# A two-layer hybrid backbone with streamed experts on one core: float32 output projection, logits from un-normalised rows, and other slots for the weight chunks

## Chip, core and metric

One NeuronCore of a Trainium2 chip runs one program. The metric is device microseconds for one execution, lower is better; the time before is the median of three runs.

## What is computed

Two layers act on 256 latent tokens `x` and 256 context tokens `ctx` of width 1024, in float32. A layer is a mixer (attention, convolution, Fourier and recurrent branches, merged by sigmoid gates) and, after a post-norm, a mixture of 16 experts with a second post-norm. All six modulation vectors of a layer come from `c` (or `c_ctx`) by one matrix `ada_w`. The part that matters here:

```
merged = sum over branches of sigmoid(gate) * (branch @ w_branch)
x1  = layer_norm(alpha * x + gate1 * (merged @ w_out)) * ln1_g + ln1_b
h   = layer_norm(x1) * (1 + scale2) + shift2
aff = softmax(h @ w_router)                 # 16 experts
top_w, top_i = top_k(aff.T, 32)             # every expert picks 32 tokens of each stream
xe  = h[top_i]
ye  = (silu(xe @ w_e_gate) * (xe @ w_e_up)) @ w_e_down * top_w     # inner width 1408
out = layer_norm(alpha * x1 + gate2 * scatter_add(ye)) * ln2_g + ln2_b
```

Layer 0 does this for both streams (four tiles of 128 tokens), layer 1 for `x` alone (two tiles).

## The kernel before, in words

A layer is `mixer(l)` and then `finish(l)`. A scheduling framework orders the instructions of each engine; SP issues the weight loads in its own order and stops at the first one whose slot is not free.

`mixer` ends with `merge(b, br)`, which runs over four quarters q of the output columns: it loads `w_in` and `w_branch` of the quarter (L498, L499), splits them into two halves of precision (ACT L351, DVE L147), multiplies, and adds to `merged`, which lies in `big`.

`finish` then does, in this order:

1. Gate rows: the gate vector is spread over 128 partitions by a matmul of ones with a diagonal (`gate_rows`, tile `gps`, L998). Router weights `wr` are multiplied by the modulation (`wrm`, L1067).
2. The projection `w_out(si, q)`: per stream si and quarter q one load of 1 MB into a slot of ring1, ACT and DVE split weights and `merged` into high and low parts (`woh`, `wol`, `mh`, `ml`), and PE does three single-pass matmuls of 256 columns for each product (L1137, L1139, L1140), 384 in layer 0 and 192 in layer 1. DVE multiplies by the gate, adds the residual, and takes the statistics (L1147 to L1155).
3. `norms` (post-norm and inner norm, DVE L1009, L1010, ACT L269), then `logits`: eight transposes on PE (L1170), a copy out (`zt`), eight products with `wrm` (L1177), a bias, a transpose back.
4. `soft` and `topk`, for each stream alone: softmax, two matmuls that put tokens into columns, a copy into `cur` (L1204), four rounds of max, index and replace (L1213 to L1216), a cast (L1217), a masked copy `dm` (L1219).
5. One-hot matrices (L1239) and `gather`, matmuls with them that put the chosen rows into `xe` (tile `xp`, L1248, evicted at L1253 by DVE and at L1256 by ACT).
6. The experts: gate and up products (tile `p`, L1368), DVE and ACT make `he`, down products (tile `py`, L1406), weighting by DVE (`yt`, L1413). Every fourth expert, rows are scattered back by a matmul; behind the last one (tile `fin`, L1434) statistics and norm follow, and in layer 1 the output.

The expert weights of a layer are 192 chunks of 1408 KB (per expert four of gate, four of up, four of down), all issued by SP in `fetch` (L1093). A chunk takes a slot in one of four pools: ring1 (3, shared with all other weight loads), `ringa` (4 in layer 0, 7 in layer 1), `ringb` (3) and `ringc` (2), 12 and 15 in all. In layer 0 `ringa` is filled during the projection, one chunk each before four of its eight loads; in layer 1 before the last one. `ringb` opens when the projection's tiles are free, `ringc` when the norm's are. Then slots are reused in turn, as PE reads them out.

Some chunks of `ada_w` for layer 1 ("held" ones, of 1.5 MB) are loaded in layer 0's finish into ring slots and multiplied in between (tile `ax`, L207; ACT copy L210; transposes L228; DVE reduction L231).

Of the kernel before, what the change touches and what calls it, by code (L numbers as in the profile page):

```python
# [9 lines left out]
F32 = mybir.dt.float32  # L10
# [29 lines left out]
NRA = (4, 7)  # L40
NRB = (3, 3)
# [57 lines left out]
def hybrid_kernel(ctx: ExitStack, tc: tile.TileContext, out: bass.AP, A):  # L99
# [230 lines left out]

    def mixer(l, tail=None):
# [77 lines left out]
        else:  # L409
# [4 lines left out]
            def front(t):  # L414
                s = t // 2
                z = z2[:, 2 + t % 2, :]
                if s == 0:
                    post_ln(big[:, t, :], lng, lnb, big[:, t, :])
                    ln_act(z, big[:, t, :])
# [69 lines left out]
        def merge(b, br):  # L489
# [3 lines left out]
            for q in range(4):  # L493
# [6 lines left out]
                ada_more(AKEEP[l])  # L500
                for i in range(2):
# [479 lines left out]
        fills.append(merge(0, mbr))  # L981
# [10 lines left out]
    def gate_rows(pool, l, v, s):  # L992
        g = pool.tile([128, D], F32, name=f"gate{s}", tag=f"g{s}")
        for half in range(2):
            ps = pmm("gps")
# [3 lines left out]
            S.activation(out=g[:, 512 * half:512 * half + 512], in_=ps, func=AF.Copy)  # L999
        return g  # L1000
# [12 lines left out]
    def finish(l, merged):  # L1013
# [9 lines left out]
        z2 = mp.tile([128, nt, D], F32, name="z2") if both else big[:, 0:2, :]  # L1023
        idxb = mp.tile([128, ns, NE * CAP], F16, name="idxb")
        wix = mp.tile([128, NE + 8], F32, name="wix")
        iota = mp.tile([128, 2 + SEQ], F32, name="iota")
        nc.scalar.dma_start(out=iota, in_=A["k_iota"])
        rst = ExitStack()
        ringa = rst.enter_context(tc.tile_pool(name=f"ringa{l}", bufs=NRA[l], side="right", reuse_waits="tile"))
# [14 lines left out]
        cur = rp.tile([64, 256], F32, name="cur")  # L1044
        lnx = ExitStack()
# [6 lines left out]
        shw = np_.tile([128, ns, NE], F32, name="shw")  # L1052
        shb = np_.tile([16, 2], F32, name="shb")
        wpx = ExitStack()
        wp = wpx.enter_context(tc.tile_pool(name=f"wout{l}", bufs=1, side="left", reuse_waits="tile"))
        wrs = wp.tile([128, KD, NE], F32, name="wrs")
        mp2 = mp.tile([128, 16, 2], F32, name="mp2")
        pq = ptp()
        for h in range(2):
            for kk in range(2):  # L1060
# [4 lines left out]
                      in_=pq[:, 0:32].rearrange("p (k a s) -> p a k s", k=2, s=2))  # L1065
        for si, s in enumerate(streams):
            V.tensor_tensor(out=wrm[:, si], in0=wr, in1=md[:, 32:40, s:s + 1].to_broadcast([128, KD, NE]), op=ALU.mult)  # L1067
            V.tensor_tensor(out=wrs, in0=wr, in1=md[:, 24:32, s:s + 1].to_broadcast([128, KD, NE]), op=ALU.mult)
            V.tensor_reduce(out=shw[:, si, :], in_=wrs.rearrange("p k e -> p e k"), axis=AX.X, op=ALU.add)
            sp = ptp()  # L1070
            T.matmul(sp[0:16, 0:1], lhsT=shw[:, si, :], rhs=ones[:, 0:1], start=True, stop=True)
            V.tensor_copy(out=shb[:, si:si + 1], in_=sp[0:16, 0:1])
        mh = wp.tile([128, KD, N], F32R, name="mh")
        ml = wp.tile([128, KD, N], F32R, name="ml")

        def halves(j):
            S.activation(out=mh[:, j, :], in_=merged[:, j, 0:N], func=AF.Copy, scale=0.5)
            V.scalar_tensor_tensor(out=ml[:, j, :], in0=merged[:, j, 0:N], scalar=0.5, in1=mh[:, j, :].bitcast(F32),
                                   op0=ALU.mult, op1=ALU.subtract)

        chunks = []
        for e in range(NE):
            for name in ("w_e_gate", "w_e_up"):
                for kc in range(4):
                    chunks.append(A[name][l, e, 256 * kc:256 * kc + 256, :].rearrange("(p k) n -> p (k n)", k=2))
            dn = A["w_e_down"][l, e].rearrange("(p k) n -> p (k n)", k=FF // 128)
            for kc in range(4):
                chunks.append(dn[:, MSLOT * kc:MSLOT * kc + MSLOT])
        ready = []

        def fetch():
            v = slot()[:, 0:MSLOT]
            nc.sync.dma_start(out=v, in_=chunks.pop(0))  # L1093
            ready.append(v)

        def chunk():
            if not ready:
                fetch()
            return ready.pop(0)

        if both:
            y = z2
        else:
            y = big[:, 2:4, :]
        stats = {}
        gate1 = {}

        def w_out(si, q):
            s = streams[si]
            v = load(A["w_out"][l], KD, [(256 * q, 256 * q + 256)])  # L1110
            if both and q == 0:
                name = ("ctx", "x")[s]
                nc.sync.dma_start(out=z2[:, 2 * s:2 * s + 2, :], in_=A[name][0].rearrange("(t p) d -> p t d", p=128))
            if both and (si, q) in ((0, 1), (0, 3), (1, 1), (1, 3)):
                prefetch(ringa, 1)
            if not both and q == 3:
                prefetch(ringa, NRA[l])
            c = slice(256 * q, 256 * q + 256)
            ps = pax("wo").rearrange("p (i c) -> p i c", i=2)
            for k0 in (0, 4):  # L1120
                wh = wp.tile([128, 4, 256], F32R, name="woh", bufs=2)
                wl = wp.tile([128, 4, 256], F32R, name="wol", bufs=2)
                for k in (0, 2):
                    if si == 0 and q == 0:
                        halves(k0 + k)
                        halves(k0 + k + 1)
                    src = v[:, k0 + k:k0 + k + 2, :]
                    S.activation(out=wh[:, k:k + 2, :], in_=src, func=AF.Copy)
                    lo_part(V, wl[:, k:k + 2, :], src, wh[:, k:k + 2, :])
                if si == 0 and q == 0 and k0 == 0:  # L1130
                    for g in streams:
                        gate1[g] = gate_rows(wp, l, 2, g)
                for i in range(2):
                    tt = slice(128 * (2 * si + i), 128 * (2 * si + i) + 128)
                    for k in range(4):
                        o = ps[:, i, :]
                        T.matmul(o, lhsT=mh[:, k0 + k, tt], rhs=wh[:, k, :], start=(k0 + k == 0 and i == 0), stop=False,  # L1137
                                 skip_group_check=True)
                        T.matmul(o, lhsT=mh[:, k0 + k, tt], rhs=wl[:, k, :], start=False, stop=False, skip_group_check=True)  # L1139
                        T.matmul(o, lhsT=ml[:, k0 + k, tt], rhs=wh[:, k, :], start=False, stop=(k0 + k == KD - 1),  # L1140
                                 skip_group_check=True)
            if q == 0:
                stats[si] = [small.tile([128, 4, 6], F32, name="st") for _ in range(2)]
            tm = wp.tile([128, 2, 256], F32, name="tm", tag="tm", bufs=2)
            g1 = gate1[s][:, c]
            if q < 3:
# [18 lines left out]
        def logits(si, i):  # L1165
# [14 lines left out]
            if i == 0:  # L1180
                lgt[si] = pmm("lgt")
# [338 lines left out]
```

## Time and profile before

| what | us |
|---|---|
| median of three runs (2405.01 to 2407.66) | 2406.28 |
| the profiled execution | 2407.04 |
| its span, from the first to the last instruction | 2405.3 |
| PE busy | 2039.1 (85%) |
| PE weight loads busy (beside PE) | 1203.1 (50%) |
| DVE busy | 1009.3 (42%) |
| ACT busy | 638.9 (27%) |

The mean granted clock of TensorE is 0.901 of 2.4 GHz. The program moves 713 MB, 296 GB/s over the span. PE, PEld, DVE, ACT, POOL are the engines of the profile; "SPq" rows are DMA issues of SP, whose duration is the time that SP spent on them, with the waits between if a row merges several. A row "x4" merges four instructions. A name in brackets with an arrow is what ended the idle time. A float32 matmul is two instructions in these rows, a single-pass one is one.

### The profile page before, as it was taken

To read this page: it belongs to the slowest core of one execution; us is meant where nothing else is said; L and a number is where in the kernel's file an instruction comes from. 1 tells how busy PE (TensorE), PEld (TensorE's weight loads), DVE (VectorE), ACT (ScalarE), POOL (GpSimd) and SP (SyncE) were. 2 spreads that over 40 slices of the span, in tenths; PEclk is the share of its full clock that TensorE was granted. 3 is DMA by queue.
4 is the path that set the end of the run, shared out by engine and by line. 5 is a ranking of instruction groups with operands and counts; after the bars stand their busy time and mean duration, and the time that the engine had idled before them with its cause. 6 is when DMAs were issued, how large, how long until landed. Compare 5 with 4: busy or idle time off the path is not lost.

```text
span 2405.3 us, 35167 instructions
## 1 busy us (share of the span) xinstructions
PE 2039.1 (85%) x14813; PEld 1203.1 (50%) x14813; DVE 1009.3 (42%) x2063; ACT 638.9 (27%) x1165; POOL 42.5 (2%) x112
## 2 busy tenths in 40 slices
PE   7999999999989897897988798899976766767665
PEld 4877777767844332332432487788942211312111
DVE  5878855563851131311211777897641110101102
ACT  4355555453420000000000447766410000000000
POOL 1010000000000000000000000000000000000000
PEclk9999999999999999999999999999986665766668
DMA  9564533314589999999999584343799999999997
GB/s 282 162 188 149 177 102 114 90 62 172 167 314 423 419 423 423 423 422 422 423 423 422 152 257 151 98 126 117 275 369 423 423 423 423 423 423 423 424 422 302
DMA packets 226781, 713.07 MB, mean 296 GB/s; under 512 B 34428, under 2 KB 174188, under 8 KB 177472
## 3 DMA queue, kind: packets, MB, share of 16 engines
q1 hardware_dynamic: 219696, 703.37, 75.6%
q0 software_dynamic: 2528, 3.99, 0.5%
q10 hardware_dynamic: 4400, 3.47, 0.5%
q8 instruction: 116, 1.90, 0.3%
q14 instruction: 41, 0.34, 0.0%
HBM read 709.74 MB, written 1.05 MB: 296 GB/s over the span
## 4 chain that ended last, share of the span: by engine, by line
DMA 46%; PE 41%; DVE 6%; ACT 5%; issue 1%; ACTq 0%; DVEq 0%; SPq 0%
DMA wslot<-in_w_e_down_dram 16%; DMA wslot<-in_w_e_up_dram 15%; DMA wslot<-in_w_e_gate_dram 14%; PE mm L150 6%; PE mm L152 6%; PE mm L151 6%; PE p L1368 4%; PE py L1406 2%; PE pp L152 2%; PE pp L150 2%; PE pp L151 2%; PE ax L207 1%; PE sc L928 1%; PE po L953 1%; PE wo L1139 1%
## 5 line engine op out<-in xcount | busy, mean ns | idle before, releaser
L1368 PE MATMUL p<-wslot,xe 128*32 128x352 f32 x6144 | 609.4, 541 | 163.1 <-DMA wslot<-in_w_e_gate_dram 86.4
L1368 PEld LDWEIGHTS p<-wslot,xe 128*32 128x32 f32 x6144 | 201.9, 121 | 558.3 <-issue 256.4
L1406 PE MATMUL py<-wslot,ht 128*32 128x256 f32 (+2 forms) x2176 | 283.9, 492 | 87.1 <-DMA wslot<-in_w_e_down_dram 45.8
L1381 DVE TENSOR_TENSOR he<-he,p 128x352 f32<-128x352 f32 x48 | 24.3, 507 | 677.6 <-PE p L1368 677.6
L150 PE MATMUL mm<-hh,wh 128*128 128x512 f32 (+2 forms) x832 | 296.8, 358 | 6.4 <-ACT wh L351 4.6
L152 PE MATMUL mm<-hh,wl 128*128 128x512 f32 (+2 forms) x832 | 291.7, 351 | 8.8 <-DVE wl L147 8.8
L151 PE MATMUL mm<-hl,wh 128*128 128x512 f32 (+2 forms) x832 | 291.6, 351 | 0.0
L1380 ACT ACTIVATE he<-p 128x352 f32<-128x352 f32 x48 | 22.2, 463 | 964.7 <-PE p L1368 962.6
L351 ACT ACTIVATE wh<-wslot 128x512 fp32r<-128x512 f32 (+1 forms) x288 | 175.5, 624 | 251.3 <-PE mm L151 168.1
L147 DVE TENSOR_TENSOR wl<-wslot,wh 128x512 fp32r<-128x512 f32 (+1 forms) x288 | 193.9, 681 | 110.8 <-ACT wh L351 106.8
L1406 PEld LDWEIGHTS py<-wslot,ht 128*32 128x32 f32 (+1 forms) x2176 | 111.0, 130 | 253.3 <-issue 94.3
L1413 DVE SCALAR_TENSOR_TENSOR yt<-py,wix,gate 32x512 f32<-32x512 f32 (+1 forms) x128 | 78.6, 614 | 304.9 <-PE py L1406 303.4
L150 PEld LDWEIGHTS mm<-hh,wh 128*128 128x128 f32 (+1 forms) x832 | 157.2, 189 | 42.4 <-issue 9.3
L152 PEld LDWEIGHTS mm<-hh,wl 128*128 128x128 f32 (+1 forms) x832 | 157.5, 189 | 33.1 <-DVE wl L147 11.0
L151 PEld LDWEIGHTS mm<-hl,wh 128*128 128x128 f32 (+1 forms) x832 | 157.6, 189 | 24.2 <-issue 3.2
L542 DVE SCALAR_TENSOR_TENSOR conv<-up,prm,conv 128x512 f32<-128x512 f32 (+1 forms) x240 | 146.3, 612 | 2.2
L150 PE MATMUL pp<-bh,wh 128*128 128x512 f32 (+1 forms) x256 | 87.1, 342 | 2.6 <-ACT bh L528 1.4
L152 PE MATMUL pp<-bh,wl 128*128 128x512 f32 (+1 forms) x256 | 86.5, 339 | 1.9 <-DVE wl L147 1.9
L151 PE MATMUL pp<-bl,wh 128*128 128x512 f32 (+1 forms) x256 | 86.2, 337 | 0.0
L1256 ACT ACTIVATE xe<-xp,mp 128x128 f32<-128x128 f32 x48 | 21.9, 457 | 175.2 <-PE xp L1248 96.0
L1139 PE MATMUL wo<-wol,mh 128*128 128x256 f32 x192 | 55.5, 290 | 3.2 <-DVE wol L147 2.8
L1137 PE MATMUL wo<-woh,mh 128*128 128x256 f32 x192 | 55.8, 292 | 0.0
(385 smaller groups left out, 2413.3 us busy)
## 6 DMA issues: line engine op xcount, KB each, us to landing
wslot<-in_w_e_gate_dram SPq DMA_DIRECT2D x128, 1408.0 KB, 27.1
wslot<-in_w_e_up_dram SPq DMA_DIRECT2D x128, 1408.0 KB, 27.1
wslot<-in_w_e_down_dram SPq DMA_DIRECT2D x128, 1408.0 KB, 27.1
wslot<-in_ada_w_dram SPq DMA_DIRECT2D x26, 1536.0 KB, 7.9
wslot<-in_w_in_dram SPq DMA_DIRECT2D x36, 1024.0 KB, 5.4
wslot<-in_w_branch_dram SPq DMA_DIRECT2D x32, 512.0 KB, 6.5
wslot<-in_w_in_dram SPq DMA_DIRECT2D x30, 512.0 KB, 5.8
wslot<-in_w_out_dram SPq DMA_DIRECT2D x12, 1024.0 KB, 5.2
```

The lines of the kernel that those rows point to most:

```text
L147: eng.tensor_tensor(out=lo, in0=src, in1=hi.bitcast(F32), op=ALU.subtract)
L150: T.matmul(o, lhsT=ah, rhs=bh, start=start, stop=False)
L151: T.matmul(o, lhsT=ah, rhs=bl, start=False, stop=False)
L152: T.matmul(o, lhsT=al, rhs=bh, start=False, stop=stop)
L351: S.activation(out=a, in_=v, func=AF.Copy)
L542: V.scalar_tensor_tensor(out=cv, in0=up[:, :, k:k + 256], scalar=pm[:, ct, R_CVW + k:R_CVW + k + 1], in1=cv, op0=ALU.mult, op1=ALU.add)
L1137: T.matmul(o, lhsT=mh[:, k0 + k, tt], rhs=wh[:, k, :], start=(k0 + k == 0 and i == 0), stop=False, skip_group_check=True)
L1139: T.matmul(o, lhsT=mh[:, k0 + k, tt], rhs=wl[:, k, :], start=False, stop=False, skip_group_check=True)
L1368: T.matmul(ts[si][32 * q:32 * q + 32, 0:FB], lhsT=xe[:, k, el, 32 * si:32 * si + 32], rhs=v[:, kk, FB * q:FB * q + FB], start=(k == 0), st ...
L1381: V.tensor_tensor(out=hs, in0=hs, in1=pss[1][si][:, 0:FB], op=ALU.mult)
L1406: T.matmul(py[M * u:M * u + M, c:c + 256 * n], lhsT=ht[:, k], rhs=v[:, 256 * (i - 11 * kc):256 * (i - 11 * kc + n)], start=(k == 0), stop= ...
L1413: V.scalar_tensor_tensor(out=yt[s][32 * el:32 * el + 32, c], in0=py[ps_, 0:dw], scalar=wix[ps_, e:e + 1], in1=gate2[ps_, :], op0=ALU.mult, ...
```

## The change

- **Projection.** `w_out` is loaded once per layer, in four chunks of 512 columns (three in ring1, the fourth, `wo3`, in a tile of its own), and multiplied plainly: float32 matmuls of 512 columns, 64 in layer 0 and 32 in layer 1. Splits, `mh`, `ml` and the stream-wise reloads are gone. The factor 0.5 goes into the gate row. The sum is kept in `y`, in layer 0 a tile of its own.
- **Logits.** Transposes (`turn`) take `y` before the norm. The norm's scale and bias are folded into `wrm` and four constants per expert (`cst`, made by a few DVE operations and one matmul per stream), and four small DVE steps per tile apply mean and reciprocal. `normed`, on ACT, writes the normalised rows for the gather.
- **Softmax and top-k** run once for both streams, on 48 partitions; both gathers follow it.
- **Slots.** `ringa` 5 and 9, `ringb` 2 and 1. In layer 0 `ringa` opens before the last branch is merged, and `merge` asks for two chunks per quarter (five in all); in layer 1 all nine are asked for behind `w_out`'s loads.
- **Held chunks.** Two in tiles of their own, loaded at the start of the finish, two in ring1 behind the projection.
- **Last chunk** of each layer's stream: three loads (1024, 1024, 768 columns).
- **Last expert of layer 1**: the residual and experts 12 to 14 are added to the result early; the last one's weighting is one step of 128 partitions on DVE (before four of 32), followed by eight matmuls of 256 columns (before four of 512). Its scatter matrix `cml` is made in a spare slot.

```diff
-NRA = (4, 7)
-NRB = (3, 3)
+NRA = (5, 9)
+NRB = (2, 1)
...
+    def fetch():
+        v = slot()[:, 0:MSLOT]
+        src = moe["chunks"].pop(0)
+        for c0, c1 in ([(0, 1024), (1024, 2048), (2048, MSLOT)] if not moe["chunks"] else [(0, MSLOT)]):
+            nc.sync.dma_start(out=v[:, c0:c1], in_=src[:, c0:c1])
+        moe["ready"].append(v)
...
-        def merge(b, br):
+        def merge(b, br, ahead=0):
...
                 ada_more(AKEEP[l])
+                if ahead:
+                    prefetch_a(l, ahead)
...
+        y = mp.tile([128, nt, D], F32, name="y") if both else big[:, 2:4, :]
+        z2 = big if both else big[:, 0:2, :]
+        res = y if both else big
...
+        for half in range(2):
+            for kh in range(2):
+                src = A["w_out"][l, 512 * kh:512 * kh + 512, :]
+                if half and kh:
+                    wpc[kh, half] = wp.tile([128, 4, 512], F32, name="wo3")
+                    nc.sync.dma_start(out=wpc[kh, half], in_=src[:, 512:1024].rearrange("(k p) n -> p k n", p=128))
+                else:
+                    wpc[kh, half] = load(src, 4, [(512 * half, 512 * half + 512)])
...
+        prefetch_a(l, NRA[l])
...
+        for _ in range(2 if both else 0):
+            hl_, hp_ = ada_q.pop(0)
+            hn = sum(c1 - c0 for c0, c1 in hp_)
+            hv = wp.tile([128, KD, 384], F32, name="held", bufs=2)[:, :, 0:hn]
...
+        def w_out(t, half):
+            acc[t, half] = pmm("wo")
+            tt = slice(128 * t, 128 * t + 128)
+            for k in range(KD):
+                T.matmul(acc[t, half], lhsT=merged[:, k, tt], rhs=wpc[k // 4, half][:, k % 4, :], start=(k == 0),
+                         stop=(k == KD - 1))
...
+        def turn(t, j0):
+            tp = ptp()
+            for j in range(j0, j0 + 4):
+                T.transpose(tp[:, 128 * (j - j0):128 * (j - j0) + 128], y[:, t, 128 * j:128 * j + 128], ident)
+            zt = zts[t, j0] = np_.tile([128, 4, 128], F32, name="zt", bufs=4)
+            S.activation(out=zt, in_=tp.rearrange("p (a b) -> p a b", a=4), func=AF.Copy)
...
+            u = lv[:, t, :]
+            V.scalar_tensor_tensor(out=u, in0=cst[:, si, 0, :], scalar=ln1[t][0], in1=lg, op0=ALU.mult, op1=ALU.add)
+            V.scalar_tensor_tensor(out=u, in0=u, scalar=ln1[t][1], in1=cst[:, si, 2, :], op0=ALU.mult, op1=ALU.add)
+            V.scalar_tensor_tensor(out=u, in0=cst[:, si, 1, :], scalar=ln2[t][0], in1=u, op0=ALU.mult, op1=ALU.add)
+            V.scalar_tensor_tensor(out=u, in0=u, scalar=ln2[t][1], in1=cst[:, si, 3, :], op0=ALU.mult, op1=ALU.add)
...
+        for t in range(nt):
+            w_out(t, 0)
+            if t:
+                turn(t - 1, 4)
+            evict(t, 0)
+            if t:
+                norms(t - 1)
+            w_out(t, 1)
+            if t and t < nt - 1:
+                logits(t - 1)
+            turn(t, 0)
+            evict(t, 1)
+        turn(nt - 1, 4)
+        norms(nt - 1)
+        warm(AF.Exp, ln2[nt - 1][1])
+        logits(nt - 2)
+        logits(nt - 1)
+        for r in held:
+            ada_use(*r)
+        held = [ada_load(*ada_q.pop(0)) for _ in range(min(AHELD - 2, len(ada_q)))]
         wpx.close()
...
+                if e == NE - 1 and not both:
+                    V.scalar_tensor_tensor(out=yl, in0=py[:, 0:dw], scalar=wix[:, e:e + 1], in1=gate2, op0=ALU.mult,
+                                           op1=ALU.mult)
+                    break
```

How the order of the engines moves is shown at three places. First SP around layer 0's finish. `w_in` and `w_branch` are the mixer's weights, `w_e_gate`, `w_e_up` and `w_e_down` the expert chunks in the order of the stream. Before:

```order
L498 DMA wslot<-in_w_in_dram 128x8x256
L499 DMA wslot<-in_w_branch_dram 128x4x256
L1093 DMA wslot<-in_w_e_gate_dram 128x2816 x3
L133 DMA wslot<-in_w_out_dram 128x8x256 x3
L1113 DMA z_5051<-in_ctx_dram 128x2x1024
L1113 DMA z_5051<-in_x_dram 128x2x1024
L133 DMA wslot<-in_w_out_dram 128x8x256 x5
L133 DMA wslot<-in_ada_w_dram 128x8x384 x3
L1093 DMA wslot<-in_w_e_up_dram 128x2816
L133 DMA wslot<-in_ada_w_dram 128x8x384
L1093 DMA wslot<-in_w_e_up_dram 128x2816 x3
L1093 DMA wslot<-in_w_e_down_dram 128x2816 x4
```

Now:

```order
L351 DMA wslot<-in_w_e_gate_dram 128x2816 x4
L351 DMA wslot<-in_w_e_up_dram 128x2816
L543 DMA wslot<-in_w_in_dram 128x8x256
L544 DMA wslot<-in_w_branch_dram 128x4x256
L133 DMA wslot<-in_w_out_dram 128x4x512 x3
L1115 DMA wo_5105<-in_w_out_dram 128x4x512
L1120 DMA y<-in_ctx_dram 128x2x1024
L1120 DMA y<-in_x_dram 128x2x1024
L1132 DMA held<-in_ada_w_dram 128x8x384 x2
L133 DMA wslot<-in_ada_w_dram 128x8x384 x2
L351 DMA wslot<-in_w_e_up_dram 128x2816 x3
L351 DMA wslot<-in_w_e_down_dram 128x2816 x4
```

Five chunks instead of one now stand ahead of the last `w_in` and `w_branch`; the eight `w_out` loads are four (the fourth, `wo_5105`, is `wo3`); the residual `y` and the two held chunks follow, and ahead of the other seven of the first twelve chunks (three `up`, four `down`) two `ada_w` loads, where there were four.

Second PE at the start of layer 0's finish, behind the last product of the merge (`pp`). `lnr` holds the norm's scale and bias as rows, `cat` the sums that become the constants. Before:

```order
L152 MATMUL pp<-bh,wl 128x512
L1061 MATMUL tp<-mods_112,c_ident 64x16 x4
L998 MATMUL gps<-dg,ones 128x512 x4
L1137 MATMUL wo<-woh,mh 128x256
L1071 MATMUL tp<-ones,shw 16x1
L1139 MATMUL wo<-wol,mh 128x256
L1140 MATMUL wo<-woh,ml 128x256
L1137 MATMUL wo<-woh,mh 128x256
```

Now:

```order
L152 MATMUL pp<-bh,wl 128x512
L1141 MATMUL tp<-mods_112,c_ident 64x16 x4
L1182 MATMUL wo<-wslot,big 128x512 x2
L1047 MATMUL gps<-dg,ones 128x512 x2
L1182 MATMUL wo<-wslot,big 128x512 x2
L1150 MATMUL tp<-c_ident,lnr 128x16
L1182 MATMUL wo<-wslot,big 128x512 x2
L1047 MATMUL gps<-dg,ones 128x512 x2
L1182 MATMUL wo<-wslot,big 128x512 x2
L1171 MATMUL tp<-cat,ones 128x64
L1182 MATMUL wo<-wslot,big 128x512 x4
```

The projection starts before the gate rows, in products of 512 columns, and the matmuls of the constants (`cat`) stand between them.

Third DVE in layer 0, from the copy of the scores into `cur` on. `tp` in `adared` rows is a held chunk's result, `pb` the spread indices, `xe` a step of the gather. Before, for the second stream:

```order
L1204 COPY cur<-pa 16x256
L1213 MAX wi<-cur 16x8
L231 TENSOR_REDUCE adared<-tp 128x6
L1214 MAX_INDEX ix<-wi,cur 16x8
L237 TENSOR_TENSOR mods_121<-adared,adab_117 128x6
L1239 TENSOR_SCALAR oh<-pb,iota 128x128
L1216 MATCH_REPLACE cur<-wi,cur 16x256
L1239 TENSOR_SCALAR oh<-pb,iota 128x128
L1213 MAX wi<-cur 16x8
L1253 TENSOR_SCALAR xe<-xp,mp_5091 128x4x32
L1214 MAX_INDEX ix<-wi,cur 16x8
L1216 MATCH_REPLACE cur<-wi,cur 16x256
```

Now, for both streams:

```order
L1267 COPY cur<-pa 16x256 x2
L1274 MAX wi<-cur 48x8
L1275 MAX_INDEX ix<-wi,cur 48x8
L1277 MATCH_REPLACE cur<-wi,cur 48x256
L1274 MAX wi<-cur 48x8
L231 TENSOR_REDUCE adared<-tp 128x6
L1275 MAX_INDEX ix<-wi,cur 48x8
L237 TENSOR_TENSOR mods_121<-adared,adab_117 128x6
L1277 MATCH_REPLACE cur<-wi,cur 48x256
L1274 MAX wi<-cur 48x8
L1275 MAX_INDEX ix<-wi,cur 48x8
L231 TENSOR_REDUCE adared<-tp 128x6
```

The steps of the gather (`oh`, `xe`) stood between those of the top-k; now all of them stand behind it.

## Rows read from the trace of the kernel before

**Rows 1.** The page, part 4: the chain that ended last, shares by engine and line.

```profile
DMA 46%; PE 41%; DVE 6%; ACT 5%; issue 1%; ACTq 0%; DVEq 0%; SPq 0%
```

**Rows 2.** Windows: busy us of PE, PEld, DVE, ACT, POOL, then PEclk, DMA share, GB/s.

```profile
705.00:1330.00 625.00, 548.47 (x5092) 225.48 (x5092) 119.66 (x224) 33.11 (x65) 6.55 (x13) 0.99 1.01 419
1336.00:1340.00 4.00, 3.31 (x8) 1.12 (x6) 3.92 (x7) 0.00 (x0) 0.00 (x0) 1.00 1.04 328
1743.00:1753.00 10.00, 0.39 (x3) 0.26 (x2) 9.62 (x20) 2.02 (x4) 0.00 (x0) 0.61 0.89 356
```

**Rows 3.** Timeline of SP, layer 0: start, us, engine, line, operation, tiles, count.

```profile
704.13 11.23 SPq L1093 DMA_DIRECT2D wslot<-in_w_e_gate_dram  x4
717.40 2.69 SPq L1093 DMA_DIRECT2D wslot<-in_w_e_up_dram  x2
```

**Rows 4.** Chain of waits, layer 0's finish: start, us, what.

```profile
662.72 0.76 DVE tm L1153 x2
...
674.14 1.97 PE tp L1170 x8
...
682.17 1.92 PE lg L1177 x16
...
689.35 0.43 DVE cur L1204
...
698.57 0.17 DVE wi L1217
...
704.05 1.14 PE xp L1248 x8
...
705.19 2.50 PE p L1368 x30
```

**Rows 5.** Timeline of PE's weight loads after layer 0's last chunk.

```profile
1337.44 0.19 PEld L1434 LDWEIGHTS fin<-yt,cm 128*128 128x128 f32 x1 [0.24 <-issue]
1337.87 0.19 PEld L1434 LDWEIGHTS fin<-yt,cm 128*128 128x128 f32 x1 [0.24 <-issue]
```

**Rows 6.** Timeline of PE: first instruction of layer 0's finish.

```profile
592.07 0.43 PE L1061 MATMUL tp<-mods,c_ident 128*64 128x16 f32 x8
```

**Rows 7.** Timeline of DVE: router weights of layer 0, idle before and releaser in brackets.

```profile
601.48 0.29 DVE L1067 TENSOR_TENSOR wrm<-wr,mods 128x128 f32<-128x128 f32 x1 [1.88 <-DMA wr<-in_w_router_dram]
```

**Rows 8.** Chain of waits, layer 1's finish: start, us, what.

```profile
1718.20 1.91 PE gps L998 x4
...
1743.17 0.76 DVE tm L1153 x2
...
1746.85 1.30 DVE big L1010
...
1748.17 1.30 DVE st L253 x2
...
1762.50 0.20 DVE rmx L1193
...
1764.52 0.43 DVE cur L1204
...
1770.46 0.18 DVE wi L1217
```

**Rows 9.** Timeline of SP, layer 1: the last two free slots and first reuses.

```profile
1746.46 30.84 SPq L1093 DMA_DIRECT2D wslot<-in_w_e_gate_dram  x4
```

**Rows 10.** Timeline of ACT: last quarter of layer 0's merge, first split.

```profile
567.47 0.63 ACT L351 ACTIVATE wh<-wslot 128x512 fp32r<-128x512 f32 x1 [1.60 <-PE pp L151]
```

**Rows 11.** Timelines: PE and DVE behind the last chunk of layers 0 and 1.

```profile
1331.98 2.79 PE L1406 MATMUL py<-wslot,ht 128*64 128x256 f32 x12 [0.65 <-DMA wslot<-in_w_e_down_dram]
...
2389.72 1.50 PE L1406 MATMUL py<-wslot,ht 128*32 128x256 f32 x22 [1.90 <-DMA wslot<-in_w_e_down_dram]
...
2391.28 2.00 DVE L1413 SCALAR_TENSOR_TENSOR yt<-py,wix,gate 32x256 f32<-32x256 f32 x4 [12.25 <-PE py L1406]
```

**Rows 12.** The page, part 6: DMA issues, KB each, us to landing.

```profile
wslot<-in_w_branch_dram SPq DMA_DIRECT2D x32, 512.0 KB, 6.5
```

More of the change, by code (lines that the diff above doesn't have):

```diff
@@ L980, in mixer @@
             ic.__exit__(None, None, None)
-        fills.append(merge(0, mbr))
+        if both:
+            moe_stream(l)
+        fills.append(merge(0, mbr, 2 if both else 0))
         fill(100)
@@ L1089, in finish @@
[L1089 to L1146, printed above, removed]
-                V.tensor_tensor(out=tm, in0=ps, in1=g1.unsqueeze(1).to_broadcast([128, 2, 256]), op=ALU.mult)
-                yq = y[:, 2 * si:2 * si + 2, c]
-                V.scalar_tensor_tensor(out=yq, in0=yq, scalar=ALPHA, in1=tm, op0=ALU.mult, op1=ALU.add)
-            for i in range(2):
-                yq = y[:, 2 * si + i, c]
-                if q == 3:
-                    V.tensor_tensor(out=tm[:, i, :], in0=ps[:, i, :], in1=g1, op=ALU.mult)
-                    V.scalar_tensor_tensor(out=yq, in0=yq, scalar=ALPHA, in1=tm[:, i, :], op0=ALU.mult, op1=ALU.add)
-                V.bn_stats(out=stats[si][i][:, q, :], in_=yq)
@@ new lines, in norms @@
+        def norms(t):
+            mean, r = ln1[t]
+            x1 = y[:, t, :]
+            V.scalar_tensor_tensor(out=x1, in0=x1, scalar=mean, in1=lng, op0=ALU.subtract, op1=ALU.mult)
+            st = np_.tile([128, 2, 6], F32, name="stx", bufs=2)
+            for a in range(2):
+                xa = x1[:, 512 * a:512 * a + 512]
+                V.scalar_tensor_tensor(out=xa, in0=xa, scalar=r, in1=lnb[:, 512 * a:512 * a + 512], op0=ALU.mult, op1=ALU.add)
+                V.bn_stats(out=st[:, a, :], in_=xa)
+            ln2[t] = moments(st, "x")
@@ new lines, in finish, with logits @@
+        lv = rp.tile([128, nt, NE], F32, name="lv")
+        def logits(t):
+            si = t // 2
+            lg = pax("lg")[:, 0:NE]
+            for j in range(KD):
+                T.matmul(lg, lhsT=zts[t, j // 4 * 4][:, j % 4, :], rhs=wrm[:, si, j, :], start=(j == 0), stop=(j == KD - 1))
+            u = lv[:, t, :]
[3 more added lines that the diff above has]
+            V.scalar_tensor_tensor(out=u, in0=u, scalar=ln2[t][1], in1=cst[:, si, 3, :], op0=ALU.mult, op1=ALU.add)
@@ L1204, in soft @@
-            V.tensor_copy(out=cur[r0:r0 + 16, :], in_=pa[r0:r0 + 16, 0:256])
-            return af[:, 1, 0:1]
-        def topk(si):
-            s = streams[si]
-            r0 = 32 * s
-            ix = rp.tile([64, CAP], U32, name="ix", bufs=2)
+            for t in range(nt):
+                r0 = 32 * streams[t // 2]
+                T.matmul(pa[r0:r0 + 16, 128 * (t % 2):128 * (t % 2) + 128], lhsT=af[:, t, :], rhs=ident, start=True,
+                         stop=True, skip_group_check=True)
@@ L1386, in finish @@
                             total[t, c.start] = pmm("fin")
-                            T.matmul(total[t, c.start], lhsT=ident, rhs=big[:, t, c], start=True, stop=False)
+                            for h in range(1 if both else 2):
+                                d = c if both else slice(c.start + 256 * h, c.start + 256 * h + 256)
+                                o = total[t, c.start][:, d.start - c.start:d.stop - c.start]
+                                T.matmul(o, lhsT=ident, rhs=res[:, t, d], start=(h == 0), stop=False, skip_group_check=not both)
                 if e == 0:
```

273 lines of the change are left out of this document (164 added, 109 removed).

## Prediction

> **What bounds the kernel now.** The chain that ended last, summed by engine, comes first: it is almost half DMA, by far the most of it expert weights, and 41% PE [rows 1]. So two kinds of time count: the weight streams, and what runs on PE, DVE and ACT before a stream is at full speed or after it has ended. Second, the windows: in layer 0's stream, 705 to 1330, the 16 DMA engines are never free and move 419 GB/s, while PE at a granted clock of 0.99 is busy 548 of 625 us [rows 2]. A chunk of 1408 KB at that rate is 3.44 us. There, nothing but an earlier start or a shorter end helps.
>
> When does the stream start? Twelve chunks fit into the slots of layer 0 (fifteen in layer 1); SP issues the next one when PE has read the first out of its slot. The SP rows give these releases: the first four chunks from 704.13, the next at 717.40 [rows 3]. The four cover 13.27 us, about their 13.8 us of DMA, and from there PE frees a slot faster than DMA fills one (the four's rows of PE are 2.50 us of expert matmuls and 1.14 us of gather each [rows 4]). **So the issue at 717.40 is the mark: as much earlier as it comes, so much earlier layer 0 ends.** What leads up to it are the projection (last column out at W = 662.72), the router chain (scores in `cur` at 689.35), the top-k (through at 698.57), and gather and first chunks [rows 4].
>
> **The projection.** Before: three single-pass matmuls per product, with the splitting on ACT and DVE. After: plain float32 matmuls of 512 columns, 64 in layer 0 and 32 in layer 1. The trace has that shape at layer 0's end: one float32 matmul is two instructions, and their weight loads start 0.43 us apart [rows 5], in a window whose granted clock is 1.00, the 2.4 GHz level [rows 2]. So one costs 0.86 us. The Trainium skill (TensorE: Matmul & The Clock Gate, Back-to-back issue gap) counts N/2.4 + 2.5 ns for N columns at the full clock, 216 ns here, and no more for float32; by it the projection would be half as long. The row says double that; I go by the row, and the page's figure is the last rival.
>
> Layer 0 from 592.07, where PE begins the finish [rows 6]: 64 x 0.86 = 55.0; four gate matmuls 3.4; six groups of four transposes at 1.0 (eight instructions took 1.97 at one place [rows 4], where PE had just been idle; that is the other end) 6.0; logits of two tiles at 1.92 [rows 4] 3.8; constants 0.7. One new wait: PE stands in order behind the matmul of the folded constants, which needs `wr` (DVE got it at 601.48, after 1.88 us of waiting for it) and some ten small DVE operations at 0.29 [rows 7], so 604.4. PE, with eight projection and four gate matmuls in front, is there by 603. I take 2.5 us for it and other small waits; ends 0 and 6, the latter if the loads of `y` and of the held chunks, new on SP's queue at that time, push `wr` back. Sum 592.1 + 55.0 + 3.4 + 6.0 + 3.8 + 0.7 + 2.5 = **663.5, 0.8 later** than before. The splits that vanish from ACT and DVE are worth nothing in themselves: PE sets the pace.
>
> Layer 1 from 1718.2 [rows 8]: gate rows 1.9, 32 x 0.86 = 27.5, two groups of transposes 2.0, constants 0.7: 1750.3 where it was 1743.17, **7.1 later**.
>
> **The router chain.** Before, norm, transposes and logits of the last tiles follow one another behind W: 689.35 - 662.72 = 26.6 us in layer 0, 1764.52 - 1743.17 = 21.4 in layer 1 [rows 4, 8]. After, the transposes take the un-normalised rows and the norm enters the logits as four small DVE steps, so transposes and logits lie beside the norm. What remains behind W on DVE, by layer 1's rows: eviction, three steps like its first of 0.76, 2.1; moments with ACT's root 0.8, two scalings at 1.30, statistics 1.30 [rows 8], moments again 0.8; up to eight logit steps at about 0.2 between them, 1.6; softmax to the copy 1764.52 - 1762.50 = 2.0 [rows 8] and the copy 0.43. That is 11.6. In layer 0 a second copy, reductions of the two held chunks that stand ahead of the last reciprocal in DVE's order, and their waits for PE bring it to 15.5 (ends 13 and 21: the reductions free, or PE's held matmuls at half clock); in layer 1 I take 12.8. So the chain is **11.1 shorter in layer 0, 8.6 in layer 1**.
>
> **Top-k, gather, first chunks.** Layer 0 did top-k for each stream, the first stream's gather interleaved with the second's top-k: 9.2 us from the copy to its end [rows 4]. Now one top-k holds both streams, 5.9 us as in layer 1 (1764.52 to 1770.46 [rows 8]) and 0.3 for two adaLN reductions: 3.0 saved. But the first stream's gather loses its cover: one-hots and masks of two streams behind it, 1.2; the first eviction, 0.9; and PE must do 16 instead of 8 gather instructions ahead of each of the first four chunks, 4 x 1.14 = 4.6 [rows 4]. Net 3.7 lost. Layer 1 has one stream and does what it did.
>
> So the mark of layer 0 moves by 11.1 - 0.8 - 3.7 = **6.6 earlier**, that of layer 1 by 8.6 - 7.1 = **1.5 earlier** (1777, the end of the fourth issue there [rows 9]).
>
> **Moves on the queues.** Five chunks instead of one go ahead of the last `w_in` and `w_branch` of the mixer: 5 x 3.44 = 17 us of DMA from about 530. I put 0 on it: ACT splits the first of these weights at 567.47 [rows 10], some 15 us after that; if they were late, up to 5 us. The two held chunks in own tiles load at the start of the finish instead of behind it; two more in ring1, then ringb: SP waits there in order, for PE to have used the held chunks. All this ends before the mark, so 0, with the 21 above as the price where not.
>
> **The ends of the streams.** Layer 0's last chunk used to be consumed in one go after landing, 2.79 us [rows 11]; now the last of three pieces holds 3 of 11 blocks: 1.8 saved. Layer 1: 1.50 us likewise [rows 11], 1.1 saved, and four steps of 2.00 us in all, of which the first matmul waited for two, become one of 0.4 to 0.5: 0.5 saved. The eight extra matmuls ahead of it lie in the waits for DMA. Together **3.4** (ends 0 and 4.5). The Trainium skill (DMA: Bandwidth & Descriptors, Bandwidth) wants at least 1 MiB per transfer and gives 78% of the peak at 1 MB, 32% at 64 KB; pieces of 384 to 512 KB would lie between, and by that most of the 3.4 would go. The trace's 512 KB loads take 6.5 us to landing beside other traffic [rows 12]; the pieces are queued right behind full transfers, and I take no loss.
>
> **The sum.** 6.6 + 1.5 + 3.4 = 11.5 us. Profiled execution 2407.04, which is 0.76 above the median of the three runs: 2407.04 - 11.5 - 0.76 = **2394.8**, 0.5% below 2406.28.
>
> **Rivals.** All hang on one thing: which share f of the chain's shortening is real. Total gain = (11.1 + 8.6)f - 0.8 - 3.7 - 7.1 + 3.4 = 19.7f - 8.2. About 0.2%, 4.8 us, is what can be told from no change.
> - *Forecast*, f above 0.66: gain over 4.8. For it: transposes and logits stood on the chain one after the other, at a lowered clock. With the ends of the other terms (wait 0, gathers hidden, chain 13): 2386.
> - *Given back*, f from 0.17 to 0.66: about 2406. PE would be nearly empty behind W, as in 1743 to 1753, where it was busy 0.39 of 10 us and the granted clock 0.61, a mix of the two levels [rows 2]; logits, held matmuls and gather would then take up to twice their time.
> - *Slower*, f under 0.17: 2409 to 2414.5, at f = 0. One mechanism: the chain behind the projection is set by DVE's steps and hand-overs between engines, which remain, the transposes were beside it anyhow; then layer 1 pays its 7.1 us in full and layer 0 its lost cover. It decides where less than 3.4 of 19.7 us is saved. Against it: in layer 1 the DVE finishes its norms and then PE's transposes and logits follow, up to the softmax at 1762.50.
> - *Page's rate*: matmuls at 0.216 us would end the projection 27 and 14 us earlier; the gain would be some 50, about 2354. The weight loads speak against it.
> - *Not as it says*: the pieces of the last chunk land together; 2398, inside the forecast.
>
> **Chances.** Forecast 0.67, given back 0.19, slower 0.12, page's rate 0.02. So faster 0.69, same 0.19, slower 0.12. The range leaves out the page's rate, the lowest tenth and the worst of the slower case: 2385 to 2409.
>
> **What would show it.** Right: weight loads of `wo` 0.43 us apart; projection ends near 663.5 and 1750; `cur` copied near 679 and 1763; top-k of 6 us; fifth issue past the slots near 711, in layer 1 the first at 1775; after the last landing 1.8 and 1.6 us less. Wrong: projection instructions near 0.2 us; a DVE wait for PE of many us in front of the softmax; SP late with chunks in front of the first releases; `merge` waiting for `w_in`.

## The result, and the profile after

The changed kernel takes 2393.33 us (median of five runs, 2391.43 to 2394.99) against 2406.28: the ratio is 0.9946 with a 95% interval of 0.9935 to 0.9957. The forecast was 2394.8, with a range of 2385 to 2409. The profiled execution is one of 2391.89 us, with a span of 2390.1. Two later executions, one of `oldlast` (2484.54 us) and one of the kernel before (2680.80 us), showed a lower mean granted clock (0.789 and 0.722) than all others (0.895 to 0.907) and are left out of every median below.

The chain that ended last, on the page, now has more PE than DMA [rows 1]:

```profile
PE 44%; DMA 43%; DVE 6%; ACT 5%; issue 1%; ACTq 0%; DVEq 0%; SPq 0%
```

The windows (columns as in [rows 2]) are layer 0's stream, in a window set 6 us to the left of that in [rows 2], and the ten microseconds behind layer 1's projection.

```profile
699.00:1324.00 625.00, 546.53 (x5087) 226.19 (x5089) 119.47 (x223) 33.11 (x65) 6.54 (x13) 0.99 1.00 419
1739.00:1749.00 10.00, 5.11 (x38) 4.76 (x36) 8.12 (x25) 4.14 (x9) 0.00 (x0) 0.66 0.79 304
```

The stream itself is what it was: PE 547 of 625 us, 419 GB/s. In the second row PE, which had 0.39 us of work there [rows 2], has 5.11: the logits now lie beside DVE's norm.

Layer 0's projection, in timelines: first PE's weight loads, then PE and DVE at its start.

```profile
616.72 0.19 PEld L1182 LDWEIGHTS wo<-wslot,big 128*128 128x128 f32 x1 [0.24 <-issue]
617.15 0.19 PEld L1182 LDWEIGHTS wo<-wslot,big 128*128 128x128 f32 x1 [0.24 <-issue]
```

```profile
590.52 0.43 PE L1141 MATMUL tp<-mods,c_ident 128*64 128x16 f32 x8
...
602.26 0.29 DVE L1162 TENSOR_TENSOR wrp<-wr,mods 128x128 f32<-128x128 f32 x1 [5.42 <-DMA wr<-in_w_router_dram]
...
605.05 0.41 PE L1171 MATMUL tp<-cat,ones 128*128 128x64 f32 x2 [3.07 <-DVE cat L1160]
```

The loads are 0.43 us apart, as forecast. PE waits 3.07 us for the constants. From here to the first reuse of a slot, first the chain of waits, then DVE in a timeline, then SP:

```profile
590.72 11.52 DMA wr<-in_w_router_dram
...
605.46 5.18 PE wo L1182 x8
...
610.81 3.49 PE wo L1182 x8
...
654.74 6.87 PE wo L1182 x16
661.61 0.44 PE tp L1230 x4
662.05 2.58 PE lg L1240 x24
...
674.43 0.83 PE pa L1264 x6
...
683.18 0.18 DVE wi L1278
...
685.34 2.07 PE xp L1312 x8
...
688.05 1.71 PE xp L1312 x8
```

```profile
672.08 0.18 DVE L231 TENSOR_REDUCE adared<-tp 128x6 f32<-128x24 f32 x1 [2.19 <-PE tp L228]
672.18 0.15 DVE L1193 RECIPROCAL rsx<-sdx 128x1 f32<-128x1 f32 x1
...
675.58 0.84 DVE L1267 COPY cur<-pa 16x256 f32<-16x256 f32 x2 [1.30 <-PE pa L1264]
...
678.97 0.18 DVE L231 TENSOR_REDUCE adared<-tp 128x6 f32<-128x24 f32 x1 [0.60 <-PE tp L228]
...
681.60 0.18 DVE L231 TENSOR_REDUCE adared<-tp 128x6 f32<-128x24 f32 x1 [0.56 <-PE tp L228]
```

```profile
650.90 3.80 SPq L133 DMA_DIRECT2D wslot<-in_ada_w_dram  x2
658.21 13.69 SPq L351 DMA_DIRECT2D wslot<-in_w_e_up_dram  x3
677.78 4.85 SPq L351 DMA_DIRECT2D wslot<-in_w_e_down_dram  x4
697.93 10.64 SPq L351 DMA_DIRECT2D wslot<-in_w_e_gate_dram  x4
710.60 0.33 SPq L351 DMA_DIRECT2D wslot<-in_w_e_up_dram  x1
```

Sixteen instructions, eight matmuls, take 6.87 us: 0.859 each. W is 661.6. A held chunk's reduction (`adared`) stands ahead of the last reciprocal (`rsx`), and two more stand between steps of the top-k, which runs from the copy into `cur` (675.58) to the cast into `wi` (683.18). The mark, the fifth issue into a reused slot, has moved from 717.40 to 710.60 [rows 3].

Layer 1: the chain of waits, SP, and the end of the program (timeline of PE and DVE).

```profile
1707.72 1.72 PE gps L1047 x4
...
1731.85 6.87 PE wo L1182 x16
...
1739.15 2.59 PE lg L1240 x24
...
1750.42 0.43 DVE cur L1267
...
1756.29 0.18 DVE wi L1278
```

```profile
1702.28 7.27 SPq L351 DMA_DIRECT2D wslot<-in_w_e_gate_dram  x4
...
1711.98 29.56 SPq L351 DMA_DIRECT2D wslot<-in_w_e_down_dram  x4
1741.62 22.04 SPq L351 DMA_DIRECT2D wslot<-in_w_e_gate_dram  x4
```

```profile
2375.86 0.63 PE L1481 MATMUL py<-wslot,ht 128*32 128x256 f32 x6 [0.34 <-DMA wslot<-in_w_e_down_dram]
2376.55 0.48 DVE L1485 SCALAR_TENSOR_TENSOR wslot<-py,wix,gate 128x256 f32<-128x256 f32 x1 [10.03 <-PE py L1481]
2377.19 3.69 PE L1519 MATMUL fin<-wslot 128*128 128x256 f32 x16 [0.69 <-DVE wslot L1485]
```

W, the end of the last projection group, is 1738.7 here. From the gate rows to the first reuse (the fourth issue of the last row) it was 1718.20 to about 1777.0 [rows 8, 9], 58.8 us; now it is 1707.72 to 1763.3, 55.6 us.

### The profile page after: what moved, and what is told of

Its sections match the earlier page's. It is cut to its first block, busy times and chain, and to the rows that moved or that the text cites. A ratio compares the mean times of both kernels' runs of the same rounds, so it can differ in the third digit from the quotient of the medians.

```text
span 2390.1 us, 34384 instructions
## 1 busy us (share of the span) xinstructions
PE 2046.7 (86%) x14473; PEld 1176.3 (49%) x14473; DVE 972.6 (41%) x1996; ACT 604.3 (25%) x1104; POOL 46.0 (2%) x119
## 4 chain that ended last, share of the span: by engine, by line
PE 44%; DMA 43%; DVE 6%; ACT 5%; issue 1%; ACTq 0%; DVEq 0%; SPq 0%
DMA wslot<-in_w_e_up_dram 17%; DMA wslot<-in_w_e_down_dram 14%; DMA wslot<-in_w_e_gate_dram 10%; PE mm L150 6%; PE mm L152 6%; PE mm L151 5%; PE p L1428 4%; PE py L1481 4%; PE wo L1182 3%; PE pp L152 2%; PE pp L150 2%; PE xp L1312 2%; PE pp L151 2%; PE ax L207 1%; PE sc L975 1%
## 5 line engine op out<-in xcount | busy, mean ns | idle before, releaser
L1312 PEld LDWEIGHTS xp<-oh,big 128*128 128x128 f32 x384 | 57.5, 222 | 35.5 <-issue 16.9
L1312 PE MATMUL xp<-oh,big 128*128 128x128 f32 x384 | 67.3, 325 | 6.8 <-ACT xe L1320 3.8
```

Source lines behind the costliest of these rows:

```text
L1312: T.matmul(ps[:, 0:128], lhsT=z2[:, 2 * si + i, 256 * (j // 2) + j % 2:256 * (j // 2) + 256:2], rhs=oh[i], start=(i == 0), stop=(i == 1))
```

## The experiments

All times are medians; the kernel before had 2405.0 to 2406.6 beside them. What a run shows is read against the changed kernel's 2393.33 and, where a microsecond counts, in its trace. A distance inside a trace is counted from the first instruction of that layer's finish, where the executions differ in front of it: from there to layer 0's mark the kernel before took 125.3 us, and the changed kernel takes 120.1.

**Scatter first.** `before2` is the kernel before once more, for a second profile.

> The kernel before, unchanged, for a second profile. The distance of 1.6 us that the two profiles have by 26 us, where nothing differs, and the 2.3 us that they gain in layer 1's mixer, where the order is the same, are then scatter of single executions: the second profile has them shifted by a microsecond or more. If they belong to the change, it repeats the first within 0.3 us at both places.

It took 2402.65 us (one run; span 2400.9). It stands 1.6 us ahead of the first profile by 28 us, and gains 2.2 more in layer 1's mixer, just as the changed kernel does. So differences of this size come with single executions and need not be the change's. Its SP rows:

```profile
703.06 11.23 SPq L1093 DMA_DIRECT2D wslot<-in_w_e_gate_dram  x4
716.33 5.06 SPq L1093 DMA_DIRECT2D wslot<-in_w_e_up_dram  x3
```

Its finish begins at 590.5, like the changed kernel's, so the mark moved by 716.33 - 710.60 = 5.7 us. Laid side by side, the changed kernel is 6.4 us ahead at the end of layer 0, 9.7 in layer 1's stream and 10.8 at the end: **layer 0's finish 6.4, layer 1's 3.3, the tail 1.1.** The first profile gives similar pieces, 5.3 for the mark, 3.2 and 1.5, and some 4 us of scatter on top.

Scatter can lie in the finish as well. Three later runs with the same code there (`slots1`, `onepiece`, `oldlast`) take 119.9 to 120.3 us to the mark, as the changed kernel does, but the profiled execution of `half1`, also with the same code in layer 0, takes 123.4. Its granted clock was 0.50, the 1.2 GHz level, from 667 to 672, though PE had been busy without a gap since 655; at the same place (665 to 670) the changed kernel's was 1.00. Eight logit instructions there took 1.82 us instead of 1.03.

**The order of norm and transposes.** `normfirst` puts that one thing back:

```
-            if t:
-                turn(t - 1, 4)
             evict(t, 0)
             if t:
                 norms(t - 1)
+                place(t - 1)          # ACT writes the normed rows into y
...
             if t and t < nt - 1:
+                turn(t - 1, 0)
+                turn(t - 1, 4)
                 logits(t - 1)
-            turn(t, 0)
             evict(t, 1)
...
```

Behind the loop, the transposes and logits of the last two tiles follow their norms in the same way.

> The changed kernel with the order of the finish put back in one respect: the transposes and logits of a tile wait until its rows are normed (one more ACT pass writes the normed rows in place; the arithmetic of the logits is left as it is, so they no longer stand for the reference's). Theory: taking the un-normed rows is what shortens the router chain; behind W two tiles' transposes and logits come back onto it, some 8 us in layer 0 at full price and about as much in layer 1 at half price: 10 to 14 us slower than the changed kernel, 2403 to 2407. Rival, the chain is set by DVE's steps and hand-overs and the gain came from the joint softmax and the slots: at most 3 us, 2393 to 2396.

2410.0 us (2408.52 to 2413.07), 1.0018 of the kernel before (1.0007 to 1.0028): 16.7 us slower than the changed kernel, more than the whole gain, and beyond the range that the theory gave. In the trace, layer 0's mark comes 7.8 us later behind the start of its finish, and layer 1's first reuse 7.7 us later behind its gate rows. Its chain of waits behind layer 0's W:

```profile
669.48 1.25 ACT y L1331
670.77 1.98 PE tp L1230 x8
672.88 0.58 ACT zt L1232
673.51 1.89 PE lg L1240 x8
...
676.82 1.82 PE lg L1240 x8
678.64 4.13 PE ax L207 x30
```

and its windows there:

```profile
661.00:671.00 10.00, 2.93 (x24) 2.60 (x23) 7.35 (x21) 3.20 (x6) 0.00 (x0) 0.67 0.32 133
671.00:682.00 11.00, 10.22 (x53) 6.28 (x55) 1.38 (x6) 6.14 (x8) 0.00 (x0) 0.53 0.00 0
```

First DVE does most of the work, with PE busy 2.93 of 10 us; then PE does, busy 10.22 of 11 us at a granted clock of 0.53 (nearly all of it at the 1.2 GHz level), with groups of eight logit instructions at 1.8 to 1.9 us, where such a group took 1.03 in the changed kernel. DMA moves nothing from 671 to 682, since ringb waits for the held chunks behind the logits. The extra pass on ACT (1.25 us) has its like in the kernel before. So the order of norm and transposes carries the gain: with it put back, the rest of the change comes out 4.3 us slower than the kernel before (2405.74 beside it). How that loss is shared between the projection and the joint top-k, this run does not show.

**The projection's length.** `half0` and `half1` multiply only every other block of `w_out` in one layer, so half of the products are left out; the edit is that of `half0`, `half1` has `l == 1`:

```
-            for k in range(KD):
+            ks = range(0, KD, 2) if l == 0 else range(KD)
+            for k in ks:
```

> The changed kernel, but in layer 0 the projection multiplies only every other block of rows (32 of 64 matmuls; half of the products are left out). Theory, layer 0 is bound by PE there: DMA was idle for 33 us during the projection because every slot was full or not yet free, and slots come free with the projection, so the full 32 x 0.86 = 27.5 us come off the end: 2365 to 2369. Rival, the DMA wall stands in layer 0 too (twelfth chunk landed 696.7, first reuse 697.9, only 8 us idle between): 2383 to 2387.

> The changed kernel, but in layer 1 the projection multiplies only every other block of 128 rows of w_out (16 of 32 matmuls; half of the products are left out). Theory, two walls in layer 1: the fifteenth chunk lands at 1764.0 when the first slot is reused at 1763.3, and the DMA engines were idle for only 2.6 and 0.7 us from 1703 on, so the end cannot come much more than 3.3 us earlier, though PE is 16 x 0.86 = 13.8 us sooner through: 2388 to 2391 where the changed kernel has 2393.3, with DMA never idle and the first reuse waiting. Rival, the chain through projection and router alone sets the start of the stream: 13.8 us earlier, 2379 to 2381.

`half0`: 2367.83 us, 25.5 less, of 27.5: layer 0's start hangs on PE, as the theory had it. `half1`: 2386.62 us, 6.7 less, of 13.8: neither theory nor rival (its four runs lie between 2383.59 and 2391.92, so the share is rough). Its trace stands 4.9 us behind the changed kernel's at layer 1's gate rows; counted from there, the first reuse comes 12.6 us sooner (after 43.2 us instead of 55.8), but the program ends only 7.8 us sooner. Windows of the changed kernel, ahead of the first reuse and around it, then of `half1`:

```profile
1737.00:1741.00 4.00, 4.00 (x27) 3.00 (x26) 2.20 (x7) 2.02 (x3) 0.00 (x0) 1.00 0.03 11
1762.00:1764.00 2.00, 2.00 (x16) 1.00 (x8) 0.04 (x1) 0.00 (x0) 0.00 (x0) 0.83 0.12 49
```

```profile
1708.00:1760.00 52.00, 39.13 (x232) 24.78 (x234) 32.08 (x88) 12.38 (x24) 0.00 (x0) 0.80 1.00 418
```

In the changed kernel DMA stands still for 3.9 and 1.8 us, more than the 2.6 and 0.7 of the expectation. In `half1` these gaps are gone: from 1708 on DMA is full, and what the chain is shorter beyond them is lost. So in layer 1 two bounds stand close together. A longer chain costs its full price (`normfirst`), a shorter one brings half of what it saves, or a little more.

**Slots and early loads.** `slots1` sets layer 1's slots back to 7 and 3, `noahead` takes the early requests out of layer 0's merge:

```
-NRA = (5, 9)
-NRB = (2, 1)
+NRA = (5, 7)
+NRB = (2, 3)
```
```
-        fills.append(merge(0, mbr, 2 if both else 0))
+        fills.append(merge(0, mbr, 0))
```

> The changed kernel with layer 1's slots as before the change: ringa 7 and ringb 3 instead of 9 and 1, so two chunks more wait for the end of the projection. Theory, two walls in layer 1: DMA loses 2 x 3.4 us beside the projection, and the end comes 5 to 7 us later, 2398 to 2401. Rival, layer 1 is bound by the router chain and the loads are hidden: no change, 2392 to 2395.

> The changed kernel with nothing asked for during layer 0's merge; the five ringa chunks are issued in the finish, behind w_out and the residual. Theory: DMA is idle for 33 us during the projection, so the five chunks, 17 us, load there at no cost: within 1.5 us of 2393.3. Rival, the early request is where layer 0's gain comes from: 2400 or more.

2393.45 and 2392.77 us: neither matters. For `noahead` that was the theory. For `slots1` the theory fell: a slot of ring1 takes the eighth chunk during the projection, so only one chunk is later. DMA then stands still for some 5.7 us in one piece, from 1735.3 to 1741, and not again at the first reuse: about as long as the two gaps of the changed kernel together. About 1 us is lost in its trace.

**Room for held chunks.** `noroom` loads all four into ring1 behind the projection:

```
-        for _ in range(2 if both else 0):
+        for _ in range(0):
...
-range(min(AHELD - 2, len(ada_q)))
+range(min(AHELD, len(ada_q)))
```

> The changed kernel without room of their own for held chunks: all four are loaded into ring1 behind the projection. Theory: 3 MB more to load between the projection and the first reuse, 7.3 us, where DMA had 7.9 us of idle, and the last two are used late, so down chunks wait for them: the mark comes 2 to 6 us later, 2395 to 2399, though the router chain loses its held matmuls and DVE's 2.2 us of waiting. Rival, the chain decides: 1 to 3 us earlier, 2390 to 2392.

2391.97 us (0.9946, 0.9933 to 0.9959), span 2390.2: by the medians as the change. The trace is nearer to the rival: the last of the first twelve chunks is issued some 3 us later, but the router chain, without held matmuls ahead of the softmax, is 2.1 us shorter (11.8 us from W to the first copy into `cur`, 13.9 in the changed kernel), and the mark comes after 117.9 us instead of 120.1. Two microseconds are less than the medians tell.

`heldall` and `heldfirst` go the other way and use the held chunks sooner: in `heldfirst` the two in own tiles (the edit shown), in `heldall` also the two in ring1 (ahead of `soft()`).

```
+        for r in held:
+            ada_use(*r)
         turn(nt - 1, 4)
         norms(nt - 1)
         warm(AF.Exp, ln2[nt - 1][1])
         logits(nt - 2)
         logits(nt - 1)
-        for r in held:
-            ada_use(*r)
```

> The changed kernel with the held chunks of ada_w multiplied sooner in layer 0: the two in own tiles right behind the last projection matmul, the two in ring1 before the softmax. Theory: in the changed kernel DVE waits 2.2 us for a held chunk's reduction ahead of the last reciprocal, and SP waits for the same chunks before it can issue ringb and two down chunks (DMA idle 6.5 us); without both the stream starts 2 to 4 us sooner: 2389 to 2391.5. Rival, first reuse and twelfth landing are set by something else (top-k, gather): 2392 to 2394.5.

> The changed kernel with the two held chunks of the own tiles multiplied right behind the last projection matmul, ahead of the last transposes and logits; the two in ring1 stay where they were. Theory after the two runs before: what made that order slow there was ACT, whose root for the last statistics stood behind the copies of the ring1 chunks; without those, DVE's 2.2 us of waiting goes, ringb is issued 4 us sooner, and the mark of layer 0 comes 1 to 2.5 us earlier: 2390.5 to 2392.5, and in the trace the first copy into cur near 673. Rival, another order on ACT or PE gives it back: 2393 or more.

`heldall`: 2397.97 us, 4.6 slower. The wait did not go, it went to another engine. ACT's root of the last statistics stands in its order behind the copies of the ring1 chunks, and the softmax behind a table load (chain of waits):

```profile
675.75 0.49 ACT adapart L210
676.24 0.18 ACT sdx L1191
...
676.44 1.28 ACT L1249
...
679.08 0.64 PE pa L1264 x8
```

`pa`, the softmax's result, comes 4.3 us later than in the changed kernel, once the 0.3 us between the two executions are taken off, and the mark 2.5 us later (122.6 us). The trace is 5.4 us longer than the changed kernel's; most of the rest lies in layer 1's mixer, where both do the same. `heldfirst`, without the wait on ACT, took 2392.77 us (0.9950, 0.9937 to 0.9963): no change that can be told. SP issued ringb at 664 instead of 671 as expected, but `pa` is where it was: PE's logits now come last. The mark comes after 118.0 us, 2.0 sooner, which again is less than the medians tell.

**The gather's cover.** `ctxtopk2` is `heldall` with softmax and top-k of the context stream during the projection of `x`:

```
             evict(t, 1)
+            if both and t == 2:
+                warm(AF.Sqrt, soft(0))
+                topk(0)
+                spread(0)
```

> As heldall, and softmax and top-k of the context stream run during the projection of x, so that the gather of the context stream lies beside the top-k of x again, as before the change. Theory: the prediction's term for the lost cover (3.7 us, of it 4.6 for 16 instead of 8 gather instructions per chunk) is real, and comes back on top of heldall: 2384 to 2388. Rival, DMA is then the bound of the start, or DVE is full during the projection and delays W: no better than heldall.

2394.11 us: as the changed kernel, 3.9 less than `heldall`. `pa` is 4.6 us late here too, yet the mark (710.34) is where the changed kernel has it, after 119.4 us, 3.2 sooner than in `heldall`. So the cover is worth 3 to 4 us, but this kernel pays for it on ACT.

**The ends.** `onepiece` loads the last chunks whole, `oldlast` has the old last expert in layer 1 (four steps, four matmuls; the conditions `not both` of the new code set to false).

```
-        for c0, c1 in ([(0, 1024), (1024, 2048), (2048, MSLOT)] if not moe["chunks"] else [(0, MSLOT)]):
+        for c0, c1 in [(0, MSLOT)]:
```

> The changed kernel with the last chunk of each layer's stream in one load. By the prediction's terms, 1.8 and 1.1 us come back: 2396. By the two traces (the distance between the kernels is 7.9 us before layer 0's end and 7.8 behind it) layer 0's split is worth nothing and only layer 1's 1.1 comes back: 2394 to 2395.

> The changed kernel with the last expert of layer 1 as before: four weighting steps of 32 partitions and four matmuls of 512 columns, no early addition of experts 12 to 14. By the prediction's term 0.5 us come back, behind the last landing: first final matmul 1.0 to 1.1 us behind the end of the last down product's wait chain where the changed kernel has 0.7; total 2393 to 2395. Rival, the one wide step and its scatter matrix are worth more, 1 us and over: from 2395.

2394.55 us (0.9952, 0.9938 to 0.9965) and 2394.36 us (0.9961, 0.9948 to 0.9975), both within reach of no change. In the trace of `oldlast` 0.4 us are lost behind the last down product (1.07 us to the first final matmul, 0.69 in the changed kernel). In that of `onepiece`, layer 1's tail is 0.7 us longer: from the landing of the last chunk but one to the first final matmul it takes 5.57 us instead of 4.85. The pieces themselves land hardly later, 3.52 us behind that chunk instead of 3.38. In layer 0, from the mark to the final matmuls, the three traces with a whole last chunk take 617.9 to 618.5 us, the eleven with pieces 616.4 to 618.1: 0.8 us less by their means, within what this stretch varies.

No version that makes all products beat the change by more than the measurement tells.

## Why the prediction was right

**Price and length of the projection: right, in layer 0 partly by luck.** A matmul took 0.859 us, and 0.86 was used. In layer 0 W is 71.1 us behind the finish's start, where it was 70.7: 0.4 later, 0.8 forecast. From the gate rows layer 1 took 31.0 us to W instead of 25.0: 6.0 later, 7.1 forecast. The rival that goes by the Trainium skill's rate (TensorE: Matmul & The Clock Gate, Back-to-back issue gap), 0.216 us for each of a matmul's two instructions, is ruled out by the same rows: these stand 0.43 us apart. The wait for `wr` was mis-sized. PE waited 3.07 us instead of 1.4, since the load took 11.52 us to land. In the kernel before it had taken 7.62 (chain of waits):

```profile
593.84 7.62 DMA wr<-in_w_router_dram
```

The eight instructions behind the wait then took 5.18 us, the next eight 3.49, as the granted clock was 0.81 from 605 to 614. That makes some 4.8 us, where 2.5 stood for all small waits. Six groups of four transposes, 2.7 us instead of the 6.0 forecast, made up for it.

**The router chain: right, a little too small.** From W to the first copy into `cur` 14.0 us in layer 0 (15.5 forecast, 26.6 before), in layer 1 11.7 (12.8 forecast, 21.4 before). So the chain is 12.6 and 9.7 shorter instead of 11.1 and 8.6. That the held chunks' reduction would stand ahead of the last reciprocal was seen in the order; DVE waited 2.19 us for it. The rival "slower", by which DVE's steps set the chain and the transposes lay beside it, is refuted by `normfirst`.

**Top-k, gather, first chunks: too cheap.** From the first copy to the mark it was 28.0 us, and is 35.0: 7.0 lost, not 3.7. This is the term that was mis-sized, in both of its parts. The top-k took 7.6 instead of 6.2: the two reductions in it had been priced without their waits for PE (0.60 and 0.56 us), and the second copy into `cur` falls into it. From the last cast to the mark it takes 27.4 us, 18.8 before: 8.6 lost, 6.7 forecast. The gather's first steps go one after the other before any expert matmul (14.8 us from the last cast to the first reuse, 5.6 before), and they ran at the lower of TensorE's two levels, as the rival "given back" had it: PE had waited for DVE's top-k, busy only 1.18 us from 681.6 to 685.3. Windows of the changed kernel and, for the first stream's gather, of the kernel before:

```profile
685.30:690.00 4.70, 4.66 (x19) 4.08 (x20) 3.00 (x10) 1.42 (x4) 0.00 (x0) 0.50 0.99 408
```

```profile
692.00:700.00 8.00, 5.80 (x56) 4.37 (x56) 7.24 (x24) 2.21 (x5) 0.00 (x0) 1.00 1.00 424
```

Its first two groups took 2.07 and 1.71 us, where 1.14 had been used. `ctxtopk2` gives 3 to 4 us as what the lost cover is worth.

**The marks.** Layer 0: 12.6 - 0.4 - 7.0 = 5.2, by the second profile 5.7; 6.6 forecast. Layer 1: 9.7 - 6.0 = 3.7 by the chain, of which 3.2 to 3.3 arrived; 1.5 forecast. Together 8.9, 8.1 forecast: two errors of opposite sign, and that their sum came out so near is luck.

**The ends: half.** 1.1 us in layer 1 (1.6 forecast); in layer 0 some 0.8 us at most, not clear of the scatter (1.8 forecast). The third piece is used within 0.6 us of landing in layer 1, but the gain is small beside the scatter. The sum is 6.4 + 3.3 + 1.1 = 10.8 us, the medians say 12.95, and 11.5 were forecast.

**Moves at no cost: right** for the early five chunks (`noahead`) and, by the medians, for the held chunks' room (`noroom`), which may cost some 2 us by its trace. What the prediction did not see is that in layer 1 DMA stands still for only some 6 us between 1702 and the first reuses, so that a still shorter chain would bring only a part of what it saves (`half1`).

## What to carry to other kernels

Find the work that stands behind the last matmul of a stage in a row of engines, and ask which of it needs the result that came before: here transposes and products could take un-normed rows, and that paid for a projection that became longer. Each wait removed has a successor on another in-order engine, and the orders of all engines, ACT's among them, must be read before it is taken for gone. Before costing a shorter start of a stream, count DMA's idle time up to it: it bounds what can arrive.

## What was not expected of the hardware

The router weights, 64 KB on ACT's queue, took 7.6 us to land in the kernel before and 11.5 us in the changed one, where SP's loads of `w_out`'s fourth chunk, the residual and the held chunks lie beside them. There they were issued 1.6 us earlier in the finish and landed 2.3 us later; no run tests which of the loads does it. Two executions of one program differed by 1.6 us after the first 28 us, and by 2.2 us more in layer 1's mixer. The same code of layer 0's finish took 3.3 us longer in one execution (`half1`), in which the granted clock stood at 0.50 for some 5 us although PE had been busy without a gap before.
